# Hybrid retention and attention encoder layer: partial sums by accumulating DMA, a longer ring of split operands, LN2 statistics on ScalarE, and a new product order in the first f-tile pair

## The chip, the cores and the metric

The kernel runs on one core of a Trainium2 chip. A core has five engines that work at the same time, each through a queue of its own, in order: TensorE (PE in the profile; its weight loads are shown as PEld), VectorE (DVE), ScalarE (ACT), GpSimd (POOL) and SyncE (SP), which here only issues transfers. They meet through semaphores. Transfers run on 16 DMA engines that all queues share. The metric is the device time of one execution in microseconds; the times of several runs are given as their median.

## The reference

One post-norm encoder layer for 1024 tokens of width 1024, in float32. After the projections, eight retention heads and eight windowed attention heads give `mix`, and then:

```python
h = _layer_norm(ALPHA * h + mix, ln1_gain[i], ln1_bias[i])
g = jnp.einsum('bsd,df->bsf', h, w_ffn_gate[i].astype(jnp.float32))
up = jnp.einsum('bsd,df->bsf', h, w_ffn_up[i].astype(jnp.float32))
ffn = jnp.einsum('bsf,fd->bsd', jax.nn.silu(g) * up, w_ffn_down[i].astype(jnp.float32))
...
h = _layer_norm(ALPHA * h + ffn + ple_gate * ple, ln2_gain[i], ln2_bias[i])
```

The hidden width of the feed-forward part is 2816, which is 22 tiles of 128, taken as 11 pairs. The change touches only the gate and up products of the first pair, the down product, and the second layer norm (LN2).

## The kernel before

**Split operands.** Every float32 operand is split into a rounded part and a remainder, each in a format that TensorE multiplies at full rate. `split` (L72 to L74) does it with a copy on ScalarE (L73) and a subtraction on VectorE (L74). A product then takes three matmuls (`mm3`, L76 to L79, and `mm3c`, L823 to L827, in the feed-forward part), each of 128x128 by 128x512.

**Seven products instead of eight.** The gate, up and down products use a Winograd form of Strassen's scheme: a 2x2 block product with seven multiplications, numbered 1 to 7. The left operands are blocks or sums of blocks.

**Gate and up stage.** `Pair` (L842) handles one pair of f-tiles; m = 0 is the gate weight, m = 1 the up weight (the "halves" of the prediction). A unit is one product p for one m: 12 matmuls into one PSUM bank. `gunits` (L956 to L959) lists the units; TensorE runs them in this order. `Pair.prep` (L866) splits the left operand into a buffer named `w` or `u`, by turns; its source is a weight block as loaded (`raw` or `ln`) or one of four sums in `H`, which `s_sums` (L856 to L864) makes on GpSimd. Those sums go into a buffer that the stage before uses until its last matmul. Products 1 and 2 accumulate in one bank (group 0), products 6, 7 and 4 in another, 5 and 3 in a third. `post` (L896) takes results out: after product 1 it copies the bank to `s1` on ScalarE (L910), after product 2 it applies SiLU or multiplies (L916, L918). The loop (L1160) issues the preparation of the unit seven ahead, then a unit's matmuls, then its `post`. Only TensorE's order is fixed by hand. The other engines' queues are ordered by the framework's scheduler, which ranks instructions by their place in the code and takes those that it holds ready; each engine then runs its queue in order.

**Down stage.** Here the roles turn: a unit is one product p and one pair n, with 12 matmuls over four token tiles (t = 0 to 3, four banks). Pairs are cut into two segments (5 and 6 pairs, L968). `seq` (L1115) orders products and segments; the last is product 4 of segment 1, run token tile by token tile. In all there are 77 units. `dload` (L1005) brings the left operand (ring `a`) and the weight block (ring `b` for products 2, 3 and 7; ring `chain` for 1, 5, 6 and 4, where the block is changed step by step by accumulating DMAs, L1003, on GpSimd's queue). `dprep` splits both into ring `op`: 16 tiles before, from four groups of four that become free at the end of the gate and up stage. A ring's slot is written again when its reader is done. `d_ahead` (L1152) sets how far loads and splits are issued ahead in the code.

**Results.** `accd` holds the eight token tiles (t and t + 4), loaded from memory at unit 4 (`load_acc`). `dpost` (L1073) adds each product's banks to them on VectorE (`addto`, L1054). Product 1 belongs to three quarters of the output. Segment 0's part is kept in `R` (L1081), segment 1's is added to it (L1084), and then twelve additions of half tiles on GpSimd (L1086) go through the list `later`, one per unit. When a tile is complete, `stats` (L1057) and `rstd` (L1061 to L1063) make mean and variance on VectorE and the inverse root on GpSimd, and `ln2_half` (L1067 to L1069) applies LN2 in two VectorE steps per half and stores it. Tiles 4 to 7 are complete after product 3 of segment 1, tiles 0 to 3 after product 4.

Of the kernel before, what the change touches and what calls it, by code (L numbers as in the profile page):

```python
# [9 lines left out]
F32 = mybir.dt.float32  # L10
F32R = mybir.dt.float32r
AF = mybir.ActivationFunctionType
ALU = mybir.AluOpType
# [3 lines left out]
P = 128  # L17
S = 1024
D = 1024
KT = D // P  # L20
NT = S // P
HF = 512
# [4 lines left out]
EPS = 1e-5  # L27
# [13 lines left out]
def layer(tc, xT, xn, w_first, w_mt, w_rv, w_out, w_pg, w_pe, pT, w_gu, w_dn,  # L41
          consts, dec_b, dec_c, sink, gng, lnp, out):
    nc = tc.nc
    act, dve, pool, pe, sp = nc.scalar, nc.vector, nc.gpsimd, nc.tensor, nc.sync
# [7 lines left out]
    big = cstack.enter_context(tc.tile_pool(name="big", bufs=1))  # L52
    wp = cstack.enter_context(tc.tile_pool(name="wp", bufs=4))
# [3 lines left out]
    def nm(s):  # L57
        uid[0] += 1
        return f"{s}{uid[0]}"
# [31 lines left out]
    def rawt(w):  # L91
        return wp.tile([P, w], F32, tag="raw", bufs=2, name=nm("raw"))
# [20 lines left out]
    def big16(shape=(P, 2, 2, S)):  # L113
        return big.tile(list(shape), F32R, tag="H", bufs=4, name=nm("H"))
# [22 lines left out]
    for kt in range(KT):  # L137
        r = xraw[kt]
# [25 lines left out]
        w = wf[kt % 2]  # L164
# [74 lines left out]
    for h in range(2):  # L239
        sl = slice(h * HF, (h + 1) * HF)  # L240
        b = st[1, h]
# [219 lines left out]
    class Attention:  # L461
# [56 lines left out]
        def half(self, hh):  # L518
            return self.y[:, hh * HF:(hh + 1) * HF].rearrange("p (n c) -> p n c", n=4)
# [4 lines left out]
    def ytile(k):  # L524
        ys[k] = big.tile([P, S], F32, tag="A", bufs=8, name=nm("y"))
        return ys[k]
# [39 lines left out]
    with tc.manual_schedule(engines={mybir.EngineType.PE}):  # L566
# [7 lines left out]
        r = Retention(0, ytile(0))  # L574
# [5 lines left out]
        for i in range(1, NPAIR):  # L580
            X0, X1 = X(0), X(1)
            r = Retention(i, ytile(2 * i))
# [12 lines left out]
    def ct(shape, tag, bufs=None, dt=F32):  # L595
        return cpool.tile(list(shape), dt, tag=tag, bufs=bufs, name=nm(tag))
# [3 lines left out]
    for n, k in enumerate(order):  # L600
        if n % 2 == 0:
            yp = big16()
        t = yp[:, :, n % 2, :]
# [11 lines left out]
    accs, stts = [], []  # L615
# [52 lines left out]
    for kt in range(4):  # L668
        if kt % 2 == 0:
            wbig = ct([P, 2, 2, 2, HF], ("h2", "h3")[kt // 2], dt=F32R)  # L670
        r = rawt(2 * HF)
# [50 lines left out]
    for h in range(2):  # L722
        r = rawt(D)
# [220 lines left out]
    def g_unit(n, p, m, k):  # L944
        pr = pairs2[n]

        def prep():
            if p == 1:
                pr.load(m)
            pr.prep(p, m, k)  # L950
            if p == 1:
                pr.s_sums(m)

        return prep, lambda: pr.mm(p, m), lambda: pr.post(p, m)

    for n in range(NP):  # L956
        for p in (1, 6, 5, 2, 7, 4, 3):
            for m in range(2):
                gunits.append(g_unit(n, p, m, len(gunits)))  # L959

# [9 lines left out]
    rings = {"op": [], "a": [], "chain": [], "b": []}  # L970
# [7 lines left out]
    def arena(ring, t, n):  # L978
        rings[ring] += [t[:, k] for k in range(n)]


    def arenas_a():
        arena("a", rawt(2 * HF).rearrange("p (a b) -> p a b", a=2), 2)
        arena("a", rawt(2 * HF).rearrange("p (a b) -> p a b", a=2), 2)
        for _ in range(2):
            arena("a", ct([P, 2, HF], "ln", 2), 2)

    def op_arena(t):
        rings["op"] += [t[:, k] for k in range(4)]

    def b_w(n, i, j):

# [48 lines left out]
    hs = [slice(h * HF, (h + 1) * HF) for h in range(2)]  # L1041
    accd, R, later = [], [], []

    def load_acc():
        for t in range(NT):
            x = big.tile([P, D], F32, tag="A", bufs=8, name=nm("acc"))
            sp.dma_start(x, zd[t])
            accd.append(x)
# [4 lines left out]
    def addto(t, h, b, op=ALU.add):  # L1053
        dve.tensor_tensor(half(t, h), half(t, h), b, op)  # L1054

    def stats(t, h):
        dve.bn_stats(stts[t][:, 6 * h:6 * h + 6], half(t, h))  # L1057

    def rstd(t):
        stt = stts[t]  # L1060
        dve.bn_aggr(stt[:, 12:14], stt[:, 0:12])  # L1061
        dve.tensor_scalar(stt[:, 14:15], stt[:, 13:14], EPS, None, ALU.add)
        pool.tensor_tensor(stt[:, 15:16], stt[:, 14:15], cst[:, C_MH:C_MH + 1], ALU.pow)  # L1063

    def ln2_half(t, h, eng=sp):
        x, stt = half(t, h), stts[t]
        dve.scalar_tensor_tensor(x, x, stt[:, 12:13], ln2[0][:, hs[h]], ALU.subtract, ALU.mult)  # L1067
        dve.scalar_tensor_tensor(x, x, stt[:, 15:16], ln2[1][:, hs[h]], ALU.mult, ALU.add)
        eng.dma_start(out[t][:, hs[h]], x)  # L1069

# [2 lines left out]
    def dpost(p, s, t):  # L1073

        last = s == len(SEG) - 1
        b = dbank[s, GRP[p]][t]
        if p == 1:
            if s == 0:
                if t % 2 == 0:
                    R.append(wp.tile([P, 2, HF], F32, tag="w", bufs=4, name=nm("R")))  # L1080
                act.activation(R[t // 2][:, t % 2], b, AF.Copy)  # L1081
            else:
                r = R[t // 2][:, t % 2]
                dve.tensor_tensor(r, r, b, ALU.add)  # L1084
                for tt, h, op in ((t + 4, 1, ALU.subtract), (t, 0, ALU.add), (t, 1, ALU.subtract)):
                    later.append(lambda x=half(tt, h), r=r, op=op: pool.tensor_tensor(x, x, r, op))  # L1086
        elif p == 2:
            addto(t + 4, 0, b)
            if last:
                stats(t + 4, 0)  # L1090
        elif p == 5:
            addto(t, 1, b)
        elif p == 6:
            addto(t + 4, 1, b, ALU.subtract)
        elif p == 3:
            addto(t + 4, 1, b)
            if last:
                stats(t + 4, 1)
                rstd(t + 4)
                for h in range(2):  # L1100
                    later.append(lambda h=h: ln2_half(t + 4, h))
        elif p == 7:
            addto(t, 1, b, ALU.subtract)
            if last:
                stats(t, 1)
        else:
            addto(t, 0, b)
            if last:
                stats(t, 0)
                rstd(t)  # L1110
                for h in range(2):
                    ln2_half(t, h)
# [7 lines left out]
    def d_units(p, s):  # L1120
        k, first, grp, last = (s, GRP[p]), p in (1, 5, 6), SEG[s], (p, s) == seq[-1]

        def mm(n):
            if first and n == grp[0]:
                tg = sets[which[k]]
                dbank[k] = [bank(tg[t // 2]) for t in range(4)]
            if not last:
                dmm(p, n, k, range(4), first and n == grp[0], n == grp[-1])
            elif n == grp[-1]:

                for t in range(4):
                    for q in grp:
                        dmm(p, q, k, [t], False, q == n)
                    dpost(p, s, t)

        def post(n):
            if n == grp[-1] and not last:
                for t in range(4):
                    dpost(p, s, t)

        for n in grp:
            dunits.append((lambda n=n: dload(p, n), lambda n=n: dprep(p, n), lambda n=n: mm(n), lambda n=n: post(n)))
# [5 lines left out]
    ln2 = []  # L1148
# [3 lines left out]
    def d_ahead(k, what, upto):  # L1152
        while done[what] < min(upto, ND):
            dunits[done[what]][what]()
            done[what] += 1

    with tc.manual_schedule(engines={mybir.EngineType.PE}):
        for k in range(AHEAD):
            gunits[k][0]()
        for k in range(NG):  # L1160
            if k + AHEAD < NG:
                gunits[k + AHEAD][0]()
            if k == NG - 6:
                arenas_a()
                op_arena(ct([P, 4, 2, HF], "h0a", dt=F32R))
                op_arena(big16((P, 4, 2, HF)))
                op_arena(big16((P, 4, 2, HF)))
                arena("chain", ct([P, 8, HF], "h0b"), 8)
            if k == NG - 3:
                arena("b", big.tile([P, 8, HF], F32, tag="H", bufs=4, name=nm("H")), 8)  # L1170
                arena("b", big.tile([P, 8, HF], F32, tag="H", bufs=4, name=nm("H")), 8)
            if k >= NG - 6:
                d_ahead(k, 0, k - NG + 7)
            if k >= NG - 4:
                d_ahead(k, 1, k - NG + 5)
            gunits[k][1]()
            gunits[k][2]()
        arena("chain", ct([P, 8, HF], "h2"), 8)
        op_arena(ct([P, 4, 2, HF], "h3", dt=F32R))
        for k in range(ND):  # L1180
            d_ahead(k, 0, k + 8)
            d_ahead(k, 1, k + min(7, 5 + k))
            if k == 4:
                load_acc()
            if k == ND - 24:
                for j in range(2):
                    g = ct([P, D], "u", 4)
                    sp.dma_start(g, lnp[2 + j].partition_broadcast(P))
                    ln2.append(g)
            dunits[k][2]()  # L1190
            dunits[k][3]()
            if later and k < ND - 1:
                later.pop(0)()
        while later:
            later.pop(0)()
# [86 lines left out]
```

## Time and profile before

| | us |
|---|---|
| median of 3 runs (lowest to highest) | 1240.21 (1239.68 to 1242.95) |
| the profiled execution | 1243.63 |
| its span, from first to last instruction | 1241.9 |
| down stage: first matmul of its first unit | 1015.99 |
| last matmul starts | 1231.05 |
| last VectorE step ends | 1238.5 |

The profile is of one execution. Its timeline gives for each instruction the start and duration in microseconds from the span's start, the engine, the line, the operation with its output and inputs, and in brackets how long the engine had been idle and what ended that. The view by stretches gives, after the stretch, the busy time and number of instructions of PE, PEld, DVE, ACT and POOL, then the granted clock of TensorE, the share of the DMA engines and GB/s. The view by groups gives total busy time, mean nanoseconds, and idle time before with its releasers. A transfer row gives count, size and median time from issue to landing. Matmul durations overlap, so the distance from one start to the next is what a matmul costs.

### The profile page before, as it was taken

The numbers are of one execution on the slowest core, as the hardware profiler recorded it, in microseconds if no ns is written. First come the engines' busy times: TensorE is split into PE (matmuls) and PEld (weight loads), VectorE is DVE, ScalarE is ACT, GpSimd is POOL, SyncE is SP. The second block draws the span as 40 slices with busy tenths as digits, with TensorE's granted clock in tenths as the row PEclk, the third lists the DMA queues.
The fourth block names the chain that finished last, engine by engine and source line by source line (L and its number), as shares of the span: only waits on it lengthen the run. The fifth ranks groups of instructions, "written<-read, shape, count | busy, mean of one in ns | idle before, by whom it ended". The sixth has DMA issues, their size and how long they took to land.

```text
span 1241.9 us, 16279 instructions
## 1 busy us (share of the span) xinstructions
PE 1217.5 (98%) x5987; PEld 1000.0 (81%) x5987; DVE 751.7 (61%) x1295; ACT 458.6 (37%) x848; POOL 362.8 (29%) x334
## 2 busy tenths in 40 slices
PE   8999999999999999999899999999999999999995
PEld 6887878888888888877688888888888888887884
DVE  5542467666755486883655554555544665669778
ACT  4643034444665014432333333333323334353430
POOL 2000011111010020000655646547556342335211
PEclk9999999999999999999999999999999999999998
DMA  6210010100004313032332223332133489994812
GB/s 242 82 55 1 18 34 19 35 18 25 28 18 149 117 50 105 17 119 102 123 127 94 73 89 127 127 111 87 58 127 127 148 259 332 293 312 103 215 67 95
DMA packets 54959, 134.38 MB, mean 108 GB/s; under 512 B 6624, under 2 KB 8800, under 8 KB 54880
## 3 DMA queue, kind: packets, MB, share of 16 engines
q1 hardware_dynamic: 48544, 121.81, 28.6%
q0 software_dynamic: 6336, 11.54, 5.1%
q8 instruction: 47, 0.77, 0.2%
q14 instruction: 32, 0.26, 0.1%
HBM read 104.75 MB, written 28.57 MB: 107 GB/s over the span
## 4 chain that ended last, share of the span: by engine, by line
PE 89%; DVE 6%; DMA 2%; issue 1%; POOL 1%; ACT 1%; SPq 0%; DVEq 0%; POOLq 0%; ACTq 0%
PE bmm L77 7%; PE bmm L78 7%; PE bmm L79 7%; PE bmm L826 4%; PE bmm L825 4%; PE bmm L827 4%; PE bs L827 4%; PE bs L825 4%; PE bs L826 4%; PE bt L827 4%; PE bt L825 4%; PE bt L826 4%; PE bo L825 4%; PE bo L826 4%; PE bo L827 4%; PE bs L79 2%
## 5 line engine op out<-in xcount | busy, mean ns | idle before, releaser
L77 PE MATMUL bmm<-H,w 128*128 128x512 f32 x240 | 100.9, 421 | 1.2 <-ACT H L73 1.0
L78 PE MATMUL bmm<-H,w 128*128 128x512 f32 x240 | 94.3, 393 | 1.7 <-DVE H L74 1.7
L79 PE MATMUL bmm<-H,w 128*128 128x512 f32 x240 | 94.5, 394 | 0.0
L74 DVE TENSOR_TENSOR w<-raw,w 128x512 fp32r<-128x512 f32 x80 | 61.1, 773 | 42.3 <-ACT w L73 41.3
L859 POOL TENSOR_TENSOR H<-ln 128x512 f32<-128x512 f32 x22 | 28.8, 1310 | 197.0 <-PE bo L79 112.0
L73 ACT ACTIVATE w<-raw 128x512 fp32r<-128x512 f32 x80 | 49.0, 626 | 89.3 <-PE bmm L79 33.7
L480 POOL COPY sc<-skb 128x1 f32<-128x1 f32 x64 | 15.9, 255 | 213.9 <-PE bt L501 167.3
L890 POOL TENSOR_TENSOR ev<-ev 128x512 f32<-128x512 f32 x33 | 52.7, 1598 | 68.0 <-DVE ev L905 34.6
L74 DVE TENSOR_TENSOR w<-H,w 128x512 fp32r<-128x512 f32 x44 | 40.9, 932 | 41.5 <-ACT w L73 41.0
L894 POOL TENSOR_TENSOR ev<-ev,ev 128x512 f32<-128x512 f32 x44 | 62.5, 1441 | 1.7
L74 DVE TENSOR_TENSOR u<-H,u 128x512 fp32r<-128x512 f32 x44 | 36.2, 825 | 35.7 <-ACT u L73 34.7
L77 PEld LDWEIGHTS bmm<-H,w 128*128 128x128 f32 x240 | 45.3, 189 | 12.3 <-issue 2.7
L79 PEld LDWEIGHTS bmm<-H,w 128*128 128x128 f32 x240 | 45.1, 188 | 10.0
L485 DVE CUSTOM_DVE_ANT_0 sc<-cst,bs,skb 128x384 f32<-128x384 f32 (+1 forms) x64 | 34.9, 577 | 30.2 <-PE bs L484 29.9
L73 ACT ACTIVATE w<-H 128x512 fp32r<-128x512 f32 x44 | 27.6, 630 | 68.7 <-PE bs L827 18.9
L78 PEld LDWEIGHTS bmm<-H,w 128*128 128x128 f32 x240 | 45.4, 189 | 8.4 <-DVE H L74 2.2
L489 ACT ACTIVATE sc<-sc,st 128x385 f32<-128x385 f32 (+1 forms) x64 | 37.2, 584 | 37.0 <-DVE st L487 36.6
L73 ACT ACTIVATE u<-H 128x512 fp32r<-128x512 f32 x44 | 27.6, 630 | 41.9 <-PE bmm L827 10.6
L638 POOL TENSOR_TENSOR stt<-stt,cst 128x1 f32<-128x1 f32 x8 | 11.6, 1455 | 102.4 <-DVE stt L637 102.4
L1003 POOL DMA_DIRECT2D h0b<-in_w_dn x24 | 21.3, 958 | 63.8 <-DVE h0a L74 31.6
L863 POOL TENSOR_TENSOR H<-raw,ln 128x512 f32<-128x512 f32 x22 | 36.2, 1646 | 0.0
L864 POOL TENSOR_TENSOR H<-raw,H 128x512 f32<-128x512 f32 x22 | 35.5, 1615 | 1.6
(621 smaller groups left out, 3712.9 us busy)
## 6 DMA issues: line engine op xcount, KB each, us to landing
ad<-ev SPq DMA_DIRECT2D x33, 512.0 KB, 2.9
raw<-in_w_gu SPq DMA_DIRECT2D x22, 512.0 KB, 4.7
ln<-in_w_gu SPq DMA_DIRECT2D x22, 512.0 KB, 3.5
raw<-ad SPq DMA_DIRECT2D x40, 256.0 KB, 5.7
ln<-ad SPq DMA_DIRECT2D x37, 256.0 KB, 5.3
H<-in_w_dn SPq DMA_DIRECT2D x33, 256.0 KB, 5.9
raw<-in_w_mt SPq DMA_DIRECT2D x14, 512.0 KB, 3.5
h0b<-in_w_dn POOLq DMA_DIRECT2D x24, 256.0 KB, 7.1
```

The source lines that it names most:

```text
L73: act.activation(hi, raw, AF.Copy)
L74: dve.tensor_tensor(lo, raw, hi.bitcast(F32), ALU.subtract)
L77: pe.matmul(o, lh, rh, start=start, stop=False)
L78: pe.matmul(o, lh, rl, start=False, stop=False)
L79: pe.matmul(o, ll, rh, start=False, stop=stop)
L489: act.activation(sc[g][:, :nk + 1], sc[g][:, :nk + 1], AF.Exp, bias=st_[:, 1, j, g:g + 1], accum_out=st_[:, 2, j, g:g + 1])
L825: pe.matmul(o, lh, rh, start=start, stop=False, skip_group_check=True)
L826: pe.matmul(o, lh, rl, start=False, stop=False, skip_group_check=True)
L827: pe.matmul(o, ll, rh, start=False, stop=stop, skip_group_check=True)
L863: pool.tensor_tensor(s[2], a(0, 0), a(1, 0), ALU.subtract)
L890: pool.tensor_tensor(c[:, 1, :], c[:, 0, :], c[:, 1, :], ALU.mult)
L894: pool.tensor_tensor(self.ev[dst][:, 0, :], left, right, op)
```

## The change

1. In the first f-tile pair the products run in the order 1, 2, 6, 5, 7, 4, 3 instead of 1, 6, 5, 2, 7, 4, 3.
2. The ring `op` gets 22 tiles: one group of four takes the place of eight `b` slots (`b` has 8 instead of 16), and two buffers named `u` are added. Loads are issued up to 14 units ahead (8 before), splits up to 10 (7 before).
3. P1's parts: ScalarE makes a negated copy `n` of each `R`, and twelve accumulating DMAs on GpSimd's queue add `R` or `n` to the half tiles, in place of the twelve GpSimd additions. The order within a token tile changes.
4. LN2 statistics: for all tiles but tile 3, ScalarE sums each half (a copy with an accumulated output) and then sums the squares of the half minus the mean; VectorE joins the two halves. Tile 3 keeps VectorE's statistics. The mean is stored negated, so the first step of `ln2_half` adds it.

```diff
--- before.py
+++ after.py
@@ -954,7 +954,7 @@
         return prep, lambda: pr.mm(p, m), lambda: pr.post(p, m)
 
     for n in range(NP):
-        for p in (1, 6, 5, 2, 7, 4, 3):
+        for p in (1, 6, 5, 2, 7, 4, 3) if n else (1, 2, 6, 5, 7, 4, 3):
             for m in range(2):
                 gunits.append(g_unit(n, p, m, len(gunits)))
 
@@ -985,8 +985,8 @@
         for _ in range(2):
             arena("a", ct([P, 2, HF], "ln", 2), 2)
 
-    def op_arena(t):
-        rings["op"] += [t[:, k] for k in range(4)]
+    def op_arena(t, n=4):
+        arena("op", t, n)
 
     def b_w(n, i, j):
 
@@ -1053,18 +1053,33 @@
     def addto(t, h, b, op=ALU.add):
         dve.tensor_tensor(half(t, h), half(t, h), b, op)
 
+    LAST = 3
+
     def stats(t, h):
-        dve.bn_stats(stts[t][:, 6 * h:6 * h + 6], half(t, h))
+
+        if t == LAST:
+            dve.bn_stats(stts[t][:, 6 * h:6 * h + 6], half(t, h))
+        else:
+            act.activation(ct([P, HF], "sg", 2), half(t, h), AF.Copy, accum_out=stts[t][:, h:h + 1])
 
     def rstd(t):
         stt = stts[t]
-        dve.bn_aggr(stt[:, 12:14], stt[:, 0:12])
-        dve.tensor_scalar(stt[:, 14:15], stt[:, 13:14], EPS, None, ALU.add)
+        if t == LAST:
+            dve.bn_aggr(stt[:, 12:14], stt[:, 0:12])
+            dve.tensor_scalar(stt[:, 12:13], stt[:, 12:13], -1.0, None, ALU.mult)
+            dve.tensor_scalar(stt[:, 14:15], stt[:, 13:14], EPS, None, ALU.add)
+        else:
+            dve.tensor_scalar(stt[:, 12:13], stt[:, 0:1], stt[:, 1:2], -1.0 / D, ALU.add, ALU.mult)
+            for h in range(2):
+                act.activation(ct([P, HF], "sg", 2), half(t, h), AF.Square, bias=stt[:, 12:13],
+                               accum_out=stt[:, 2 + h:3 + h])
+            dve.tensor_scalar(stt[:, 13:14], stt[:, 2:3], stt[:, 3:4], 1.0 / D, ALU.add, ALU.mult)
+            dve.tensor_scalar(stt[:, 14:15], stt[:, 13:14], EPS, None, ALU.add)
         pool.tensor_tensor(stt[:, 15:16], stt[:, 14:15], cst[:, C_MH:C_MH + 1], ALU.pow)
 
     def ln2_half(t, h, eng=sp):
         x, stt = half(t, h), stts[t]
-        dve.scalar_tensor_tensor(x, x, stt[:, 12:13], ln2[0][:, hs[h]], ALU.subtract, ALU.mult)
+        dve.scalar_tensor_tensor(x, x, stt[:, 12:13], ln2[0][:, hs[h]], ALU.add, ALU.mult)
         dve.scalar_tensor_tensor(x, x, stt[:, 15:16], ln2[1][:, hs[h]], ALU.mult, ALU.add)
         eng.dma_start(out[t][:, hs[h]], x)
 
@@ -1077,13 +1092,14 @@
         if p == 1:
             if s == 0:
                 if t % 2 == 0:
-                    R.append(wp.tile([P, 2, HF], F32, tag="w", bufs=4, name=nm("R")))
-                act.activation(R[t // 2][:, t % 2], b, AF.Copy)
+                    R.append([wp.tile([P, 2, HF], F32, tag="w", bufs=4, name=nm("R")) for _ in range(2)])
+                act.activation(R[t // 2][0][:, t % 2], b, AF.Copy)
             else:
-                r = R[t // 2][:, t % 2]
+                r, n = (x[:, t % 2] for x in R[t // 2])
                 dve.tensor_tensor(r, r, b, ALU.add)
-                for tt, h, op in ((t + 4, 1, ALU.subtract), (t, 0, ALU.add), (t, 1, ALU.subtract)):
-                    later.append(lambda x=half(tt, h), r=r, op=op: pool.tensor_tensor(x, x, r, op))
+                act.activation(n, r, AF.Copy, scale=-1.0)
+                for tt, h, x in ((t, 0, r), (t + 4, 1, n), (t, 1, n)):
+                    later.append(lambda o=half(tt, h), x=x: pool.dma_start(o, x, accum_op=ALU.add))
         elif p == 2:
             addto(t + 4, 0, b)
             if last:
@@ -1167,7 +1183,7 @@
                 op_arena(big16((P, 4, 2, HF)))
                 arena("chain", ct([P, 8, HF], "h0b"), 8)
             if k == NG - 3:
-                arena("b", big.tile([P, 8, HF], F32, tag="H", bufs=4, name=nm("H")), 8)
+                op_arena(big16((P, 4, 2, HF)))
                 arena("b", big.tile([P, 8, HF], F32, tag="H", bufs=4, name=nm("H")), 8)
             if k >= NG - 6:
                 d_ahead(k, 0, k - NG + 7)
@@ -1176,10 +1192,11 @@
             gunits[k][1]()
             gunits[k][2]()
         arena("chain", ct([P, 8, HF], "h2"), 8)
-        op_arena(ct([P, 4, 2, HF], "h3", dt=F32R))
+        op_arena(ct([P, 4, 2, HF], "h3", dt=F32R), 4)
+        rings["op"] += [ct([P, 2, HF], "u", 4, F32R) for _ in range(2)]
         for k in range(ND):
-            d_ahead(k, 0, k + 8)
-            d_ahead(k, 1, k + min(7, 5 + k))
+            d_ahead(k, 0, k + min(14, 8 + k))
+            d_ahead(k, 1, k + min(10, 5 + k))
             if k == 4:
                 load_acc()
             if k == ND - 24:
```

## The prediction

> **What bounds the kernel now.** The page comes first: who is busy, and whose work makes the chain that ended last.
>
> ```profile
> span 1241.9 us, 16279 instructions
> PE 1217.5 (98%) x5987; PEld 1000.0 (81%) x5987; DVE 751.7 (61%) x1295; ACT 458.6 (37%) x848; POOL 362.8 (29%) x334
> ...
> PE 89%; DVE 6%; DMA 2%; issue 1%; POOL 1%; ACT 1%; SPq 0%; DVEq 0%; POOLq 0%; ACTq 0%
> ```
>
> TensorE is the bound and the change removes no matmul. So the only things to win are the places where TensorE waits or runs slowly, and the stretch after its last matmul. I went through TensorE's timeline for starts more than one pitch apart; the diff touches four such places and the tail. This is the first, where the first f-tile pair begins (start, duration, idle time before and who ended it):
>
> ```profile
> 593.43 0.40 PE L825 MATMUL bmm<-h0a,u 128*128 128x512 f32 x1
> ...
> 595.95 0.39 PE L827 MATMUL bmm<-h0a,u 128*128 128x512 f32 x1
> 598.65 0.50 PE L825 MATMUL bs<-H,w 128*128 128x512 f32 x1 [2.32 <-ACT w L73]
> ...
> 602.48 0.40 PE L827 MATMUL bs<-H,w 128*128 128x512 f32 x1
> ...
> 603.65 0.39 PE L826 MATMUL bs<-H,u 128*128 128x512 f32 x1
> 604.85 0.50 PE L827 MATMUL bs<-H,u 128*128 128x512 f32 x1 [0.81 <-DVE u L74]
> 605.18 0.40 PE L825 MATMUL bs<-H,u 128*128 128x512 f32 x1
> ```
>
> The first two rows bound one unit (12 matmuls): (595.95 - 593.43) / 11 = 0.229 us a matmul, 2.75 us a unit. Against that pitch, 595.95 to 598.65 loses 2.47, the eight intervals to 602.48 lose 3.83 - 1.83 = 2.00 (0.43 to 0.6 each, though nothing is awaited), and 603.65 to 605.18 loses 1.07: place A, 5.5 us. The other three, and the tail:
>
> ```profile
> 1015.99 0.47 PE L825 MATMUL bmm<-h0a 128*128 128x512 f32 x1 [0.58 <-DVE ev L905]
> ...
> 1130.35 0.39 PE L825 MATMUL bmm<-H 128*128 128x512 f32 x1
> 1131.53 0.50 PE L826 MATMUL bmm<-H 128*128 128x512 f32 x1 [0.80 <-DVE H L74]
> ...
> 1210.11 0.39 PE L827 MATMUL bs<-h 128*128 128x512 f32 x1
> 1213.25 0.61 PE L825 MATMUL bmm<-h 128*128 128x512 f32 x1 [2.75 <-DVE acc L1054]
> ...
> 1216.97 0.39 PE L825 MATMUL bmm<-H 128*128 128x512 f32 x1
> ...
> 1231.05 0.39 PE L827 MATMUL bs<-H 128*128 128x512 f32 x1
> ```
>
> B (1016) loses 0.6 to 0.8. C (1131) loses 1.18 - 0.23 and a slow next start, 1.1. D loses 3.14 - 0.23 = 2.9 in waiting and, over the nine intervals to 1216.97, 3.72 - 2.06 = 1.7: 4.6 us. What VectorE does behind C, D and the last matmul (its timeline, with GpSimd's for C):
>
> ```profile
> 1114.66 11.59 POOL L1086 TENSOR_TENSOR acc<-acc,R 128x512 f32<-128x512 f32 x9
> 1121.22 10.25 DVE L74 TENSOR_TENSOR H<-h0b,H 128x512 fp32r<-128x512 f32 x1
> ...
> 1211.82 0.68 DVE L74 TENSOR_TENSOR H<-h,H 128x512 fp32r<-128x512 f32 x1
> 1212.42 1.28 DVE L1054 TENSOR_TENSOR acc<-acc,bmm 128x512 f32<-128x512 f32 x2
> ...
> 1231.47 0.69 DVE L1054 TENSOR_TENSOR acc<-acc,bs 128x512 f32<-128x512 f32 x1
> ...
> 1232.86 1.40 DVE L1067 SCALAR_TENSOR_TENSOR acc<-acc,stt,u 128x512 f32<-128x512 f32 x2
> 1234.18 1.41 DVE L1068 SCALAR_TENSOR_TENSOR acc<-acc,stt,u 128x512 f32<-128x512 f32 x2
> ...
> 1235.81 1.40 DVE L1067 SCALAR_TENSOR_TENSOR acc<-acc,stt,u 128x512 f32<-128x512 f32 x2
> 1237.13 1.41 DVE L1068 SCALAR_TENSOR_TENSOR acc<-acc,stt,u 128x512 f32<-128x512 f32 x2
> ```
>
> A split that takes 0.68 alone takes 10.25 while GpSimd adds P1's parts. At D the addition that frees the last product's bank comes directly behind splits: VectorE is late. In the tail it normalises tile 2 (1232.86 to 1235.50) before tile 3, whose last step ends at 1238.54, 7.1 after 1231.47.
>
> **First pair reordered (place A).** Products 2 (plain weights, no GpSimd sums) go second, to cover the sums. But product 2 of half 1 accumulates into the bank that product 1 of half 1 filled, so it must wait until ScalarE has copied that bank out (L910). In the old order four units lie between; in the new order one. ScalarE's timeline shows where that copy stands (GpSimd's last sum in the last row):
>
> ```profile
> 592.71 0.60 ACT L910 ACTIVATE ev<-bmm 128x512 f32<-128x512 f32 x1 [1.07 <-PE bmm L827]
> 597.97 1.16 ACT L73 ACTIVATE w<-H 128x512 fp32r<-128x512 f32 x2 [4.67 <-POOL H L860]
> 599.02 0.61 ACT L73 ACTIVATE w<-raw 128x512 fp32r<-128x512 f32 x1
> 602.57 1.15 ACT L73 ACTIVATE u<-H 128x512 fp32r<-128x512 f32 x2 [2.94 <-POOL H L860]
> 603.63 0.61 ACT L73 ACTIVATE u<-raw 128x512 fp32r<-128x512 f32 x1
> 604.15 0.61 ACT L73 ACTIVATE w<-H 128x512 fp32r<-128x512 f32 x1
> 604.67 0.57 ACT L910 ACTIVATE ev<-bmm 128x512 f32<-128x512 f32 x1
> 600.82 1.72 POOL L860 TENSOR_TENSOR H<-H,raw 128x512 f32<-128x512 f32 x1
> ```
>
> The second copy ran at 604.67, though its matmuls ended at 596.2 and ScalarE then idled: it stands in the queue behind every split that the code issues before it, two of which wait for GpSimd until 602.5. The new order takes the two raw splits out of this stretch (their weights are loaded and their buffers free before 597) and leaves the four sum splits, and product 7's first, ahead of the copy. If the queue keeps the code's order, as these rows do, the copy runs at 603.63 + 0.6 = 604.2. TensorE does products 1 and half 0 of product 2 until 596.2 + 2.75 = 598.9, then idles to 604.3: 5.4, plus a slow restart of 2.0 as at A now: 7.4 lost for 5.5. Bounds: 5.5 gained if the copy goes out at once, 1.9 lost so. I take the loss, because the trace has this very copy behind these very splits.
>
> **P1's parts by DMA (place C).** Removed: twelve GpSimd additions. Added: four ScalarE copies with scale -1 (0.6 each) and twelve accumulating DMAs of 256 KB on GpSimd's queue. The nearest rows are the weight accumulations on that queue, issued beside VectorE splits, and their engines' time in the 33 us from 1137:
>
> ```profile
> 1106.17 0.88 POOL L1003 DMA_DIRECT2D H<-in_w_dn  x1 [0.49 <-issue]
> q0 software_dynamic: 1693, 3.09, 52.2%
> h0b<-in_w_dn POOLq DMA_DIRECT2D x6, 256.0 KB, 6.4
> ```
>
> Issue costs 0.88 + 0.49, so twelve take 16 us of GpSimd, which has nothing else then but its other weight accumulations. The transfers take 0.522 x 33 / 12 = 1.4 us each of all engines, 17 us in a stretch that is half empty. The first addition that needs one follows product 7 at about 1114 and waits for the third DMA: 1104.8 + 2 x 1.4 + 0.9 + 6.4 = 1115, against 1118.8 now. VectorE is held no more; C's 1.1 is gained (bounds 0 and 1.1). SBUF as the source is in no row; serial landing is a rival below.
>
> **22 operand tiles, and statistics on ScalarE (place D).** A split of unit k waited for unit k - 8's matmuls; now for k - 11's, 8 us earlier. The product-2, 3 and 7 weights get 8 slots instead of 16: still eight units of lead in a row, so I price that at nothing; without that cover each 256 KB load would be late by its 6 us landing.
>
> ```profile
> 1191.00:1214.00 23.00, 20.25 (x89) 16.48 (x88) 22.06 (x43) 6.93 (x12) 3.25 (x4) 0.99 0.19 69
> L489 ACT ACTIVATION_READ_ACCUMULATOR sc<-sc,st 128x1 f32 x64 | 12.0, 188 | 0.0
> L444 ACT ACTIVATE sq<-ym 128x512 f32<-128x512 f32 x8 | 5.1, 632 | 8.1 <-DVE ym L441 7.3 <-DVE y L550 0.8
> ```
>
> VectorE is busy 22.06 of these 23 us. Four statistics (0.6 apart) move away, 2.4, and six of its twelve splits here come before the window, 3.6: 16.1 remain, done by 1207.5, while the bank needs its addition by 1210.3. D's 4.6 is gained. ScalarE takes twelve passes more of 0.63 + 0.19, 9.8, on 6.93: it fits, but VectorE's normalisation now waits for them. Bounds 0 and 4.6; I take 4.6, since the margin is 2.8.
>
> D holds a choice on the restart: 2.9 us of idling here was followed by 1.7 us of half-speed matmuls. The Trainium skill (TensorE: Matmul & The Clock Gate, HAM oscillation — how this bites in real kernels) says as a rule to keep idle gaps below about 3.4 us; by it alone A's and D's gaps would not slow the clock and D would yield 2.9. The rows decide.
>
> **Tail and B.** Tile 2's path with ScalarE, from its last matmul: addition 0.6, pass 0.8, mean 0.15, two squares 1.5, variance 0.3, power 1.0, 4.4 us, against 18 x 0.229 = 4.1 until tile 3's last matmul. So its first pair of normalising steps can run before, the second (1.3) runs beside tile 3's chain; one negation is added (0.1): 1.2 gained. Bounds: 2.6 (both pairs gone) and -0.5 (both later, and a wait). B: with fewer weight slots, fewer early loads compete; 0 to 0.8, I take 0.4.
>
> **Sum.** -1.9 + 1.1 + 4.6 + 1.2 + 0.4 = 5.4 less, from a span of 1241.9 to 1236.5. The profiled execution took 1243.63, 1.7 around its span and 3.4 above the median of the runs; taken off that median, 1240.21 - 5.4 = 1234.8.
>
> **Rivals.** *The copy goes out at once.* Then A gives 5.5: 1240.2 - 12.8 = 1227.4. For it: the same copy of half 0 went at 592.71, as its matmuls ended. Against: 604.67. Chance 0.30.
>
> *ScalarE's statistics come back late*, so the deeper ring buys nothing at D: VectorE waits there for the squares of tiles 4 to 7 by as much as it saves. Then -1.9 + 1.1 + 0 - 0.5 + 0.4 = -0.9: 1241.1. For it: every tile now crosses between the two engines three times. Against: a margin of 2.8 us. Chance 0.12.
>
> *Slower: the accumulating DMAs land one after another.* Place: the additions after product 4's first segment (about 1145), which need the tenth DMA. Landing every L us from 1104.8, it is there at 1104.8 + 10 L; VectorE stands still from 1145 and TensorE runs on 11 units ahead, 30 us. It decides from L = 7.0; at L = 8 TensorE idles 10 and restarts for 2: 1234.8 + 12 = 1246.8. For it: 6.4 to land. Against: 1.4 of engine time each. Chance 0.10.
>
> **How the numbers follow.** My forecast has 0.48, with a range of its own of 1231 to 1238 (tail and B at their bounds, A's restart). 0.3% is 3.7 us, about what a measurement of this kernel can tell from no change. Below 1236.5: all of 0.30 and three quarters of 0.48, 0.66. Within: the rest of 0.48 and most of 0.12, 0.22. Above 1243.9: 0.12. The range reaches to the early copy (1226.5) and to late statistics (1241).
>
> **What would show it.** A: the second L910 copy of the first pair behind splits of `H`, TensorE idle some 5 us near 599; wrong, if it runs near 596. C: no VectorE split over 1 us near 1121. D: no wait for an L1054 addition before the last product. Tail: tile 2's second pair alone between tile 3's steps. Wrong in whole, if TensorE waits for DMA between 1030 and 1180.

## The result and the profile after

| | before | after |
|---|---|---|
| median of 7 runs each, us (lowest to highest) | 1241.92 (1239.68 to 1243.88) | 1245.2 (1244.95 to 1249.17) |
| the profiled execution, us | 1243.63 | 1245.2 |
| its span, us | 1241.9 | 1243.3 |

The ratio after to before is 1.0032, with a 95% interval of 1.0017 to 1.0047: about 0.3% slower, where 1234.8 us and a range of 1226.5 to 1241.0 had been forecast.

The head of the page of the changed kernel, with the chain that ended last:

```profile
span 1243.3 us, 16371 instructions
...
PE 1217.9 (98%) x5987; PEld 1001.5 (81%) x5987; DVE 732.3 (59%) x1289; ACT 481.8 (39%) x908; POOL 358.7 (29%) x334
...
PE 91%; DVE 4%; DMA 2%; POOL 1%; issue 1%; ACT 1%; DVEq 0%; SPq 0%; ACTq 0%; POOLq 0%
```

VectorE has 19 us less to do, ScalarE 23 us more, and the span did not shrink. So again the places where TensorE loses time have to be listed. The view of TensorE's waits (total us, how often, the longest) begins with two:

```profile
PE bmm L825 <- ACT ev L910: 5.2, 1, 5.2
PE bmm L825 <- DVE ev L905: 4.7, 1, 4.7
```

Where they lie, and what follows them, in TensorE's timeline:

```profile
597.47 0.39 PE L827 MATMUL bmm<-h0b,w 128*128 128x512 f32 x1
603.09 0.80 PE L825 MATMUL bmm<-h0b,u 128*128 128x512 f32 x1 [5.23 <-ACT ev L910]
...
607.92 0.39 PE L827 MATMUL bmm<-h0b,u 128*128 128x512 f32 x1
...
1015.97 0.39 PE L827 MATMUL bmm<-h,u 128*128 128x512 f32 x1
1021.02 0.76 PE L825 MATMUL bmm<-h0a 128*128 128x512 f32 x1 [4.67 <-DVE ev L905]
...
1024.15 0.47 PE L826 MATMUL bs<-h0a 128*128 128x512 f32 x1
...
1215.58 0.39 PE L827 MATMUL bs<-H 128*128 128x512 f32 x1
1216.09 0.47 PE L825 MATMUL bmm<-H 128*128 128x512 f32 x1
...
1232.31 0.39 PE L827 MATMUL bs<-u,u 128*128 128x512 f32 x1
```

Against the pitch of 0.229 us, A loses 5.62 - 0.23 = 5.4 in waiting and 4.83 - 11 x 0.229 = 2.3 in the eleven slow intervals to 607.92: 7.7 for 5.5 before. B, which lost 0.6 to 0.8, now loses 5.05 - 0.23 = 4.8 and, over seven intervals, 3.13 - 1.60 = 1.5: 6.3. C is gone. Of D's 4.6 there is 0.3 left (1215.58 to 1216.09).

What held the copy at A is ScalarE's timeline:

```profile
591.52 0.60 ACT L910 ACTIVATE ev<-bmm 128x512 f32<-128x512 f32 x1 [1.06 <-PE bmm L827]
596.82 1.67 ACT L73 ACTIVATE w<-H 128x512 fp32r<-128x512 f32 x3 [4.71 <-POOL H L860]
601.40 1.15 ACT L73 ACTIVATE u<-H 128x512 fp32r<-128x512 f32 x2 [2.91 <-POOL H L860]
602.46 0.58 ACT L910 ACTIVATE ev<-bmm 128x512 f32<-128x512 f32 x1
```

The second copy stands behind five splits of GpSimd's sums and runs at 602.46, though ScalarE had nothing to do for 4.71 us before them. At B it is VectorE, and ScalarE behind it:

```profile
1009.00 0.68 DVE L905 TENSOR_TENSOR ev<-ev,bo 128x512 f32<-128x512 f32 x1
1014.34 2.93 DVE L74 TENSOR_TENSOR H<-h0b,H 128x512 fp32r<-128x512 f32 x2 [4.65 <-ACT H L73]
1018.39 0.69 DVE L74 TENSOR_TENSOR H<-h0b,H 128x512 fp32r<-128x512 f32 x1 [1.12 <-ACT H L73]
1019.00 0.68 DVE L74 TENSOR_TENSOR u<-H,u 128x512 fp32r<-128x512 f32 x1
1019.61 0.68 DVE L905 TENSOR_TENSOR ev<-ev,bo 128x512 f32<-128x512 f32 x1
1020.20 1.27 DVE L905 TENSOR_TENSOR ev<-ev,bmm 128x512 f32<-128x512 f32 x2
```

```profile
1013.67 0.63 ACT L73 ACTIVATE H<-h0b 128x512 fp32r<-128x512 f32 x1 [5.66 <-DMA h0b<-in_w_dn]
1015.70 0.63 ACT L73 ACTIVATE H<-h0b 128x512 fp32r<-128x512 f32 x1 [1.39 <-DMA h0b<-in_w_dn]
...
1017.73 0.63 ACT L73 ACTIVATE H<-h0b 128x512 fp32r<-128x512 f32 x1 [0.88 <-DMA h0b<-in_w_dn]
```

The last three gate and up additions (L905), which free the PSUM banks for the down stage, had their matmuls done by about 1016.4. They stand behind four splits of down operands that nobody needs yet, and three of these wait, through ScalarE, for weights that DMAs add up (`h0b`). The fourth goes into one of the new `u` tiles. The trace of before has the same thing in small, in VectorE's timeline: one such split waits ahead of the last three additions, and TensorE waits 0.58 for them (place B).

```profile
1013.95 0.69 DVE L74 TENSOR_TENSOR H<-h0b,H 128x512 fp32r<-128x512 f32 x1 [2.53 <-ACT H L73]
1014.56 0.68 DVE L905 TENSOR_TENSOR ev<-ev,bo 128x512 f32<-128x512 f32 x1
```

The tail, in VectorE's timeline:

```profile
1227.86 0.75 DVE L1082 SCALAR_TENSOR_TENSOR acc<-acc,stt,u 128x512 f32<-128x512 f32 x1 [0.88 <-ACT sg L1074]
...
1232.58 0.75 DVE L1082 SCALAR_TENSOR_TENSOR acc<-acc,stt,u 128x512 f32<-128x512 f32 x1 [0.88 <-ACT sg L1074]
1233.25 0.68 DVE L1054 TENSOR_TENSOR acc<-acc,bs 128x512 f32<-128x512 f32 x1
...
1238.52 1.41 DVE L1083 SCALAR_TENSOR_TENSOR acc<-acc,stt,u 128x512 f32<-128x512 f32 x2
```

From the start of the last matmul to VectorE's end it is 1238.52 + 1.41 - 1232.31 = 7.6; before, 1237.13 + 1.41 - 1231.05 = 7.5. The wait for ScalarE's squares comes once per tile, 4.72 us apart (1227.86, 1232.58), while TensorE does a tile in 18 x 0.229 = 4.1: VectorE falls behind from tile to tile.

By place the change costs 2.2 at A, 5.5 at B and 0.1 in the tail, and brings 1.1 at C and 4.3 at D: 2.4 us lost. The medians differ by 3.3 and the spans by 1.4. The first copy of the pair stage, up to which nothing was changed, runs at 592.71 before and 591.52 after, so two profiles can differ by a microsecond or more from the stages ahead; the losses by place do not carry that.

### The profile page after: what moved, and what is told of

Read it like the earlier page. It is cut to its first block, busy times and chain, and to the rows that moved or that the text cites. A ratio compares the mean times of both kernels' runs of the same rounds, so it can differ in the third digit from the quotient of the medians.

```text
span 1243.3 us, 16371 instructions
## 1 busy us (share of the span) xinstructions
PE 1217.9 (98%) x5987; PEld 1001.5 (81%) x5987; DVE 732.3 (59%) x1289; ACT 481.8 (39%) x908; POOL 358.7 (29%) x334
## 4 chain that ended last, share of the span: by engine, by line
PE 91%; DVE 4%; DMA 2%; POOL 1%; issue 1%; ACT 1%; DVEq 0%; SPq 0%; ACTq 0%; POOLq 0%
PE bmm L77 7%; PE bmm L78 7%; PE bmm L79 7%; PE bmm L825 4%; PE bmm L826 4%; PE bmm L827 4%; PE bs L825 4%; PE bs L826 4%; PE bs L827 4%; PE bt L825 4%; PE bt L827 4%; PE bt L826 4%; PE bo L825 4%; PE bo L827 4%; PE bo L826 4%; PE bs L79 2%
## 5 line engine op out<-in xcount | busy, mean ns | idle before, releaser
L74 DVE TENSOR_TENSOR w<-H,w 128x512 fp32r<-128x512 f32 x44 | 38.0, 868 | 41.4 <-ACT w L73 41.0
L74 DVE TENSOR_TENSOR u<-raw,u 128x512 fp32r<-128x512 f32 x26 | 31.4, 1209 | 10.3 <-ACT u L73 9.9
```

What stands on the lines that cost most here:

```text
L74: dve.tensor_tensor(lo, raw, hi.bitcast(F32), ALU.subtract)
```

## The experiments

The theory: B comes from the new ring alone, by the order in VectorE's queue; A from the new pair order, by the order in ScalarE's. The rivals: the statistics or the accumulating DMAs are what makes B; or the weights and sums are late for TensorE itself, so that another order would only move the wait.

**The old pair order.** The other three parts stay.

```diff
-        for p in (1, 6, 5, 2, 7, 4, 3) if n else (1, 2, 6, 5, 7, 4, 3):
+        for p in (1, 6, 5, 2, 7, 4, 3):
```

> The changed kernel with the old order of the first f-tile pair (1, 6, 5, 2, ...); the other three parts stay. Theory: the new order makes place A dearer by 2.2 us (7.7 lost instead of 5.5) and has nothing to do with place B. So TensorE loses 5.5 us near 596 to 605 again, still 6.3 near 1016 to 1024, and the time is about 2.2 us below the changed kernel's: 1243, ratio to the kernel before 1.001. Rival (the new order costs nothing, the loss at A is spread in another way): the time stays at 1245, ratio 1.0025 or more.

Median 1244.02 us, ratio to before 1.0019 (1.0006 to 1.0032). That interval overlaps the changed kernel's, so the time alone does not decide. TensorE's timeline does: A loses 5.4 again (2.71 - 0.23 after the first unit, 2.0 over the slow intervals, 1.0 at the second split), and B loses 5.5. A's extra 2.2 belongs to the pair order, B does not.

**The ring alone.** The kernel before with part 2 of the change and nothing else (22 tiles, `b` with 8 slots, loads up to 14 and splits up to 10 ahead); its core:

```diff
-                arena("b", big.tile([P, 8, HF], F32, tag="H", bufs=4, name=nm("H")), 8)
+                op_arena(big16((P, 4, 2, HF)))
...
+        rings["op"] += [ct([P, 2, HF], "u", 4, F32R) for _ in range(2)]
...
-            d_ahead(k, 0, k + 8)
-            d_ahead(k, 1, k + min(7, 5 + k))
+            d_ahead(k, 0, k + min(14, 8 + k))
+            d_ahead(k, 1, k + min(10, 5 + k))
```

> The kernel before with the 22 operand tiles and their longer lead alone. Theory: the four operand tiles that come free early let VectorE's queue take splits of down units 6, 7 and 10 ahead of the last gate/up additions; these splits wait for weights that DMAs add up. So place B loses about 6.3 us near 1016 although no other part of the change is there; C and most of D are gone by the longer lead: 5.5 more, 1.1 and 3 to 4.6 less, sum between -0.2 and +1.4 us, time 1240 to 1243. Rival (B's stall comes from ScalarE's statistics or from P1's DMAs): B loses 0.8 as before, and the time is 4 to 5.7 us below the kernel before, 1236 to 1238.

Median 1243.49 us, ratio 1.0009 (0.9999 to 1.002), just above the expected 1240 to 1243. First a row of TensorE, then of VectorE:

```profile
1018.21 0.76 PE L825 MATMUL bmm<-h0a 128*128 128x512 f32 x1 [5.09 <-DVE ev L905]
```

```profile
1011.15 3.09 DVE L74 TENSOR_TENSOR H<-h0b,H 128x512 fp32r<-128x512 f32 x2 [4.22 <-ACT H L73]
...
1016.18 0.68 DVE L74 TENSOR_TENSOR u<-H,u 128x512 fp32r<-128x512 f32 x1
1016.79 0.68 DVE L905 TENSOR_TENSOR ev<-ev,bo 128x512 f32<-128x512 f32 x1
```

The stall of B is there with the same splits ahead of L905, without ScalarE's statistics and without P1's DMAs. It loses 5.25 + 2.3 = 7.5 here. C and D are both gone, though VectorE still makes the statistics and GpSimd still adds P1's parts: the longer lead alone removes them.

**The copy first (A).** Only the order of issue changes. `issue_after` puts what its block issues on that engine behind the given instruction in the queue, without a wait; `last_on` is the latest instruction issued on an engine, here the second copy of product 1.

```diff
-        for k in range(AHEAD):
+        for k in range(4):
             gunits[k][0]()
         for k in range(NG):
-            if k + AHEAD < NG:
+            if k == 2:
+                with tc.issue_after(last_on(mybir.EngineType.Activation)):
+                    for j in range(4, 2 + AHEAD):
+                        gunits[j][0]()
+            if k >= 2 and k + AHEAD < NG:
                 gunits[k + AHEAD][0]()
```

> The changed kernel, with the splits of the first pair's sums queued behind the second copy of product 1 on ScalarE (issue order only). Theory: the copy runs as its matmuls end, near 596.5; the four units of products 1 and 2 then cover GpSimd's sums, and TensorE loses at most 0.5 us at A instead of 7.7: time 7.2 to 7.7 us below the changed kernel, about 1237.7, ratio to the kernel before 0.9965. Rival (the sums or their splits are what TensorE waits for in any case): the wait moves to the first unit of product 6, near 601 to 605, and 3 us or more of the 7.7 remain: 1241 or more.

Median 1236.67 us, ratio 0.9963 (0.9948 to 0.9977). ScalarE's timeline:

```profile
593.38 0.60 ACT L910 ACTIVATE ev<-bmm 128x512 f32<-128x512 f32 x1 [3.07 <-PE bmm L827]
595.01 0.63 ACT L73 ACTIVATE w<-H 128x512 fp32r<-128x512 f32 x1 [1.03 <-POOL H L860]
```

The copy now waits only for its matmuls, and from 584 to 612 no two starts of TensorE lie more than 0.36 apart: A loses nothing. The sums were not what TensorE waited for. The copy runs at 593.38, 3.7 after the first one at 589.71; the first copy runs 1.8 earlier here than in the changed kernel's profile, and the expected 596.5 was some 1.3 too late besides. B still loses 6.5.

**The additions first (B).** Again only the order of issue: VectorE's splits of down units 4 to 10 (not 13, as the expectation says) go behind the last L905. Buffers, ring and DMAs stay.

```diff
+        add = last_on(mybir.EngineType.DVE)
         for k in range(ND):
             d_ahead(k, 0, k + min(14, 8 + k))
+            if k < 4:
+                with tc.issue_after(add):
+                    d_ahead(k, 1, k + min(10, 5 + k))
             d_ahead(k, 1, k + min(10, 5 + k))
```

> The changed kernel, with VectorE's splits of down units 4 to 13 queued behind the last gate/up addition (issue order only); buffers, DMAs and ring stay. Theory: place B falls from 6.3 us to 0.8 or less, since the additions that free the PSUM banks wait for nothing but their matmuls: time about 5.5 us below the changed kernel, 1239.7, ratio to the kernel before 0.998. Rival (the weights that DMAs add up are late for TensorE itself): the wait moves to down units 4 to 7, near 1025 to 1040, with 3 us or more, and the time stays above 1243.

Median 1239.83 us, ratio 0.9974 (0.9962 to 0.9986). VectorE's timeline, then a row of ScalarE's, then TensorE's at the change of stage:

```profile
1011.66 0.69 DVE L905 TENSOR_TENSOR ev<-ev,bo 128x512 f32<-128x512 f32 x1 [2.03 <-PE bo L827]
1014.45 0.69 DVE L905 TENSOR_TENSOR ev<-ev,bmm 128x512 f32<-128x512 f32 x1 [2.10 <-PE bmm L827]
1017.10 0.69 DVE L905 TENSOR_TENSOR ev<-ev,bmm 128x512 f32<-128x512 f32 x1 [1.96 <-PE bmm L827]
```

```profile
1017.35 0.63 ACT L73 ACTIVATE H<-h0b 128x512 fp32r<-128x512 f32 x1 [0.35 <-DMA h0b<-in_w_dn]
```

```profile
1016.67 0.39 PE L827 MATMUL bmm<-h,u 128*128 128x512 f32 x1
1016.90 0.39 PE L825 MATMUL bmm<-h0a 128*128 128x512 f32 x1
```

Each addition now waits for its matmuls alone, and the down stage starts 0.23 after the last unit. The weights are about as late as in the changed kernel (1017.35 against 1017.73), and no wait over 0.3 us turns up further on: they were never late for TensorE.

**Both orders.** The two edits together.

> The changed kernel with both corrections of issue order: the copy ahead of the sums' splits on ScalarE, the last gate/up additions ahead of the down splits on VectorE. Theory: the two losses are separate, so both gains are had in full: A and B lose at most 0.5 us each, C and D stay gone; 7.5 and 5.4 us below the changed kernel, 1230 to 1233, ratio to the kernel before 0.991 to 0.993. Rival (the work pushed back at B is late further on once TensorE arrives there earlier): a new wait in the down stage between 1015 and 1060 takes 3 us or more, 1235 or above.

Median 1230.03 us in five runs (1229.41 to 1231.21), ratio 0.9902 (0.9887 to 0.9917): faster than both kernels; against the kernel before, 1243.26 on the same chip, the ratio is worth 12 us. A loses nothing, B and D 0.3 each, C nothing. The waits of L910 and L905 have left TensorE's list, which now begins in an earlier stage:

```profile
PE bo L129 <- POOL sq L126: 1.3, 1, 1.3
PE bt L376 <- DVE kdec L365: 0.6, 1, 0.6
```

By place that is 5.5 + 0.5 + 1.1 + 4.3 - 0.1 = 11.3 below the kernel before, within the interval.

**Both orders, statistics on VectorE.** `stats`, `rstd` and `ln2_half` as before the change.

> The kernel with both corrections of issue order, and the LN2 statistics on VectorE again as before the change. Theory: the longer lead of the splits alone removes D, so the ScalarE statistics buy nothing; they only set the tail: VectorE's last step ends 7.5 us after the start of the last matmul instead of 7.6. Time within 1 us of the kernel with both corrections. Rival (the statistics carry D, as the prediction's sum had it in part): VectorE is late by some us again, TensorE waits 2 us or more for an addition before the last product, and the time is 3 us or more above.

Median 1231.22 us in six runs, ratio 0.9908 (0.989 to 0.9927): no difference from the 0.9902 that can be told. D does not come back. The last matmul starts at 1216.49 and VectorE's last step ends at 1222.59 + 1.41: 7.5. As expected, the statistics on ScalarE buy nothing here.

**The statistics alone.** The kernel before with the new `stats`, `rstd` and `ln2_half`.

> The kernel before with the LN2 statistics on ScalarE alone. Theory (ring is what cures D): four statistics of 0.6 us leave VectorE ahead of D, against a wait of 2.9 us there; D keeps a wait of about 0.5 us, or up to 2.9 if VectorE waits for ScalarE's passes in their place; A, B and C stay as before; tail 0.1 longer; time 0 to 4 us below the kernel before. Rival (crossing between the engines makes D worse): D loses more than 4.6 us, and the time is above the kernel before.

Median 1240.99 us, ratio 0.9984 (0.9971 to 0.9997). TensorE at D:

```profile
1210.24 0.47 PE L825 MATMUL bmm<-h 128*128 128x512 f32 x1 [2.42 <-DVE acc L1054]
1210.54 0.39 PE L826 MATMUL bmm<-h 128*128 128x512 f32 x1
```

The wait falls from 2.75 to 2.42 only: taking statistics off VectorE does not cure D. The slow restart is missing in this profile, so D loses 2.6 instead of 4.6. B loses 1.3 instead of 0.6 to 0.8, again behind one split that waited, and the tail is 7.6.

**P1's DMAs alone.** The kernel before with the edit of product 1 in `dpost`.

> The kernel before with P1's parts added by accumulating DMAs alone. Theory: C goes by this part alone: no VectorE split over 1 us near 1121 and no wait of TensorE near 1131, 1.1 us less; A, B and D stay at 5.5, 0.7 and 4.6. Rival (serial landing of the accumulating DMAs): additions after 1110 wait for DMAs on VectorE, and TensorE waits between 1130 and 1180.

1241.58 us in one run, so without an interval. C is gone: no split of VectorE near 1121 takes over 1 us, and from 1017 to 1209 no two starts of TensorE lie more than 0.36 apart. A loses 5.4, B 0.9. VectorE's timeline and TensorE's:

```profile
1126.60 1.29 DVE L1054 TENSOR_TENSOR acc<-acc,bmm 128x512 f32<-128x512 f32 x2 [13.31 <-DMA acc<-R]
```

```profile
1212.72 0.47 PE L825 MATMUL bmm<-h 128*128 128x512 f32 x1 [2.74 <-DVE acc L1054]
1213.03 0.40 PE L826 MATMUL bmm<-h 128*128 128x512 f32 x1
1213.27 0.40 PE L827 MATMUL bmm<-h 128*128 128x512 f32 x1
```

The first half of the rival is there: an addition waited 13.31 us for these DMAs. But slow landing is not the cause. The third of them, which the addition needs, landed 3.6 us after its issue; what came late was the issue, since in GpSimd's in-order queue the twelve stand behind five weight accumulations, the first of which waited for a load:

```profile
1105.81 0.88 POOL L1003 DMA_DIRECT2D H<-in_w_dn  x1 [10.27 <-DMA H<-in_w_dn]
...
1116.96 0.87 POOL L1087 DMA_DIRECT2D acc<-R  x1 [1.31 <-issue]
```

The second half of the rival is not there: TensorE lost nothing, though the short ring gives it less lead than the 11 units of the prediction. D keeps its wait of 2.74, without a slow restart behind it.

## Why the prediction was wrong

The places sum to 7.8 us between the forecast (5.4 less) and what came (2.4 more): B 5.9, the tail 1.3, A 0.3 and D 0.3. The rest of the way from 1234.8 to 1245.2 is the base, 1240.21 from three runs where seven gave 1241.92, and what differs between runs.

**B: the step that failed.** The prediction said: "with fewer weight slots, fewer early loads compete; 0 to 0.8, I take 0.4." It priced the slots that `b` lost and not the tiles that `op` won at the same line. It also reasoned for the ring in its steady state ("a split of unit k waited for unit k - 8's matmuls; now for k - 11's"), where an earlier split is harmless, and never asked what is queued at the change of stage. There the old kernel's units 6 and 7 split into `h3`, which is free only when the last gate and up products are done, so their splits could not be put ahead of the last additions. The four tiles that took their place, and the `u` tiles, do not wait for those products, and the splits were put into VectorE's queue ahead of L905. An in-order queue then holds three ready additions behind a split whose weight lands at 1017.7. The ring alone has the stall, and the other order alone brings the loss from 6.3 us to 0.3, with no change to a buffer or a transfer. The bounds for B left out a loss, and no rival stood at this place, though the trace of before had one such split, behind which TensorE lost 0.6 to 0.8.

**A: right, in mechanism and nearly in size.** Forecast: the copy behind the sums' splits, 5.4 of idling and 2.0 of slow restart. Measured: 5.4 and 2.3, with the copy as what ended the wait. The rival in which it goes out at once was wrong for the code as written; with that order put in by hand A falls from 7.7 to nothing, close to the 7.4 that lay between the prediction's two cases.

**C: right, and overdetermined.** 1.1 gained. Either part suffices: with the DMAs alone no split is slow; with the ring alone, beside GpSimd's additions, splits take up to 1.8 us, none takes 10.25, and TensorE loses nothing. The slower rival, in which the DMAs land one after another, did not come: the worst wait of VectorE was 13.31 us with the short ring, from late issue, and TensorE lost nothing by it.

**D: right in size, shared out wrongly.** 4.3 gained of 4.6. The sum gave it 2.4 us of statistics and 3.6 us of splits moved off VectorE. (By its own numbers VectorE would be done by 1191.0 + 16.1 = 1207.1, not 1207.5; nothing hangs on that.) The statistics alone cut the wait by 0.33 us; the ring alone removed it. So the splits' earlier place did the work, and ScalarE's passes bought nothing beside it.

**Tail: wrong.** Forecast 1.2 gained, measured 0.1 lost, inside the bounds. The 4.4 us for a tile's way through ScalarE was set beside 4.1 of TensorE's, which it already exceeds, and as if VectorE met each tile on time. But VectorE takes one tile behind the other, 4.72 us apart with the wait for the squares, and 0.6 us more per tile add up until tile 2's first normalising step stands at 1232.58, behind the last matmul.

**The restart.** The prediction went by the rows, in which waits of 2.32 and 2.75 us were followed by half-speed matmuls. That held at A, and at B; it is not a rule for waits of this length, as the last section shows.

## What to carry to other kernels

A buffer that becomes free earlier also lets its consumer into an engine's queue earlier; at a change of stage, look at which additions that free the next stage's banks will then stand behind it, and whether it waits for a DMA. When an engine that was idle holds up another, read the order of its queue before its load: here two changes of issue order alone removed 13.7 us of losses (7.7 at A, 6.0 at B), against the 5.4 that the change itself brought at C and D. Test each part of a combined change alone, since two parts that cure the same wait hide that one of them is useless.

## What the runs showed of the hardware

Waits of nearly the same length were followed by half speed in one profile and not in another. At D the kernel before waited 2.75 us and then ran eight intervals at 0.41 to 0.43 us; with P1's DMAs alone it waited 2.74 and went on at 0.24 (1213.03 to 1213.27), and with the statistics alone likewise after 2.42. At A a wait of 2.32 was followed by half speed in all five profiles that have it. After the six waits of 4.0 to 5.2 us at A and B, the slow stretch came each time and lasted 2.7 to 4.8 us.

The granted clock accounts for all of these. Around D before, in the view by stretches:

```profile
1210.00:1213.42 3.42, 0.67 (x4) 0.28 (x3) 3.42 (x6) 0.00 (x0) 0.00 (x0) 1.00 0.39 149
1213.42:1216.83 3.41, 3.41 (x9) 2.64 (x9) 3.41 (x7) 0.00 (x0) 0.00 (x0) 0.50 0.01 4
```

At A, B and D of every profile here that slowed down, the granted clock was 0.50 for 3.41 us or for twice that. Within a profile these changes lie on one grid of 3.41 us: the slow stretches of before begin at 599.02 and 1213.42, 614.40 apart, which is 180 steps of 3.413. At these places each step of the grid in which TensorE was idle for 2.04 us or more was followed by a step at 0.50, and none with 1.74 us or less was. The wait of 2.75 lay whole in one step; the 2.74 was cut by the grid into 1.16 and 1.58, the 2.42 into 1.74 and 0.68, and each 2.32 at A had at least 2.25 in one step. So what a wait of 2 to 3 us costs depends on where the grid lies, and a single profile can't price it. The Trainium skill (TensorE: Matmul & The Clock Gate, Part 1: The HAM clock gate (the "warmup" mystery)) says that the clock follows activity in a window that runs freely, so that the point of change varies with where the work falls in it; the spread and the grid here agree.

The accumulating DMAs with SBUF as their source, for which the trace of before had no row, took 6.4 us from issue to landing in the changed kernel (median of twelve, 256 KB each) and 4.7 as the only change. The transfer rows of the two, the changed kernel first:

```profile
acc<-R POOLq DMA_DIRECT2D x12, 256.0 KB, 6.4
```

```profile
acc<-R POOLq DMA_DIRECT2D x12, 256.0 KB, 4.7
```

VectorE's splits beside them kept their 0.6 to 0.7 us, where beside GpSimd's additions one had taken 10.25 in the kernel before, and several 1.8 each with the ring alone.
